# Sums of squares by one-column matmuls in two kinds of norm, and the first token half's output chain at a higher priority

## The chip, the core and the metric

The kernel runs on one core of a Trainium2 chip. A core has TensorE (PE in the profile; its weight loads are PEld), VectorE (DVE), ScalarE (ACT) and GpSimd (POOL), each with its own instruction queue that is worked in order, and DMA queues issued by SyncE (SP). Engines wait for each other by semaphores. The metric is the device time of one execution in microseconds (us); 3045.44 is the median of three runs of the kernel before.

## The reference

Three layers run one after the other on 512 tokens of width 1024. Each has a mixer and an MLP, and every one of them is wrapped in the same two norms:

```python
u = rms_norm(h, g[0])          # before the mixer (or MLP)
u = mixer(u)                   # layer 1: hybrid; 2: attention; 3: RWKV, a recurrent mixer
h = h + rms_norm(u, g[1])      # behind it, added to the residual
u = rms_norm(h, g[2])          # before the MLP, and so on

def rms_norm(x, g):
    return x * rsqrt(mean(x * x, axis=-1) + 1e-6) * g
```

The last step of the RWKV mixer is a product with a 1024x1024 matrix `w_o`; behind it come a norm, the residual, the next norm and the MLP of the third layer. The very first operation of the whole program is the norm of the input x.

## The kernel before

Activations lie transposed: eight tiles of 128 features by 512 tokens. Most products are computed from two parts, high and low, of either operand (`split`, and `load_w` for the weights: ACT casts the high part at line 63 or 69, DVE subtracts it at line 65 or 70), three matmuls each at line 80. Norms work on two halves of 256 tokens (`HALVES`), so that the second half's norm can lie beside products of the first.

A norm over features is a sum across partitions. `SumSq.add` squares a tile on ACT and adds it on DVE into an accumulator of 128x256 (`sqa`, lines 261 to 265). `sums` then multiplies each block of 128 tokens of the accumulator, as the weights, with a column of ones (line 272), so that tokens come to lie on partitions; DVE scales (line 274), POOL takes the power -1/2 (line 275). `rstd` broadcasts the factor over the partitions again by a product with the identity (line 281) and copies it out of PSUM (line 284). `postnorm` scales the mixer's output by it (line 185), adds it to h (187) and feeds a second `SumSq` with h for the next norm; `prenorm` scales h (172) and splits it.

Three places build a `SumSq`: `l1_start` (the norm of x; both halves are spawned at once, with the same priority), `out7` at the end of the RWKV mixer (the last of eight partial products with `w_o`, line 1228, is added to y at line 1230, and y is squared), and `final` for every other mixer and MLP. `out7` hands over to `postnorm` and to the next `prenorm`, for one half and then for the other.

The order of instructions on each engine is set by a scheduler when the program is built. It goes by a priority that code asks for with `high_priority` (`ahead`); the constants `HP...` on line 17 are those priorities, and `HPO` belongs to the chains of `out7`. At run time each engine works its list in that order: an instruction that waits holds up all behind it on its engine. PSUM for products and sums comes from one pool of four tiles (`psm`), the squares' tiles from two (four in `l1_start`).

Of the kernel before, what the change touches and what calls it, by code (L numbers as in the profile page):

```python
# [8 lines left out]
F32 = mybir.dt.float32  # L9
F32R = mybir.dt.float32r  # L10
AF = mybir.ActivationFunctionType
# [2 lines left out]
PSUM = bass.MemoryType.PSUM  # L14
DRAM = bass.MemoryType.DRAM

HP, HPA, HPB, HPS, HPO, HP1, HP1B = 300, 50, 50, -300, 0, 300, 300
S = 512
D = 1024
NT = D // 128  # L20
# [4 lines left out]
class Core:  # L25
# [147 lines left out]
            self.split(t, xn[i][0][:, s0:s1], xn[i][1][:, s0:s1])  # L173
        yield

    def postnorm(self, y, q, g, s0, s1):

        nc = self.nc
        q.sums()
        yield  # L180
        rs = q.rstd()
        q2 = SumSq(self, s1 - s0)
        for i in range(NT):
            t = self.tmp.tile([128, S], F32, tag="t", name="t")[:, :s1 - s0]
            nc.vector.scalar_tensor_tensor(t, y[i][:, s0:s1], self.vec(g, i), rs, ALU.mult, ALU.mult)
            hs = self.h[i][:, s0:s1]
            nc.vector.tensor_tensor(hs, hs, t, op=ALU.add)
            q2.add(hs)
            if i % 2:
                yield  # L190
        return q2
# [58 lines left out]
class SumSq:  # L250


    def __init__(self, core, n, pool=None):
        self.c, self.n, self.acc = core, n, None
        self.pool, self.bufs = (pool, 4) if pool else (core.tmp, 2)

    def add(self, a):
        c, nc = self.c, self.c.nc
        if self.acc is None:
            self.acc = c.tmp.tile([128, S // 2], F32, tag="sqa", name="sqa", bufs=2)[:, :self.n]  # L260
            nc.scalar.activation(self.acc, a, AF.Square)
        else:
            t = self.pool.tile([128, S // 2], F32, tag="sq", name="sq", bufs=self.bufs)[:, :self.n]
            nc.scalar.activation(t, a, AF.Square)  # L264
            nc.vector.tensor_tensor(self.acc, self.acc, t, op=ALU.add)  # L265

    def sums(self):
        c, nc = self.c, self.c.nc
        nb = self.n // 128
        ps = c.psm.tile([128, S], F32, tag="mm", name="mm")  # L270
        for b in range(nb):
            nc.tensor.matmul(ps[:, b:b + 1], self.acc[:, b * 128:(b + 1) * 128], c.ones[:, 0:1], start=True, stop=True)
        self.r = c.tmp.tile([128, 4], F32, tag="r1", name="r1", bufs=4)[:, :nb]
        nc.vector.tensor_scalar(self.r, ps[:, :nb], 1.0 / D, 1e-6, ALU.mult, ALU.add)  # L274
        nc.gpsimd.tensor_tensor(self.r, self.r, c.mhalf[:, :nb], op=ALU.pow)  # L275
# [35 lines left out]
class L1:  # L311


    def l1_start(self, pool, xn, g):

        x = pool.tile([128, NT, S], F32, name="x0")
        src = self.I["x"].rearrange("i p t -> p i t")
        self.h = [x[:, i] for i in range(NT)]
        for s0, s1 in HALVES:
            def chain(s0=s0, s1=s1):  # L320
                for n in (slice(0, 4), slice(4, 8)):
                    self.nc.sync.dma_start(x[:, n, s0:s1], src[:, n, s0:s1])
                q = SumSq(self, s1 - s0, pool)
                for i in range(NT):
                    q.add(self.h[i][:, s0:s1])
                yield from self.prenorm(q, g, xn, s0, s1)
            self.spawn(self.ahead(chain(), HP1 if s0 == 0 else HP1B))
        self.pump()
# [681 lines left out]
class L3:  # L1010
# [20 lines left out]
    def l3_mixer(self, u, g_post, then):  # L1031
        nc, tc, I = self.nc, self.tc, self.I
        W = lambda n, i: I[n][i]
        with ExitStack() as lx:
# [3 lines left out]
            with tc.tile_pool(name="mx", bufs=8) as mx:  # L1038
                c0 = lp.tile([128, 6 * NT], F32, name="c0")
                a, b = VEC_AT["mu_prev"], VEC_AT["mu_next"]  # L1040
# [42 lines left out]
                for s0, s1 in SEG3:  # L1083
# [3 lines left out]
                    for m in range(NT):  # L1087
                        ps = self.psm.tile([128, S], F32, tag="mm", name="mm")[:, :s1 - s0]
# [22 lines left out]
            y, out7 = self.rwkv(lp, rkd, vm, tw, ta, sg)  # L1111
            self.unspill_h()
            for s0, s1 in HALVES:
                self.spawn(self.ahead(out7(s0, s1, g_post, then), HPO))
                next(self.bg[-1])

    def spill_h(self):
# [10 lines left out]
    def rwkv(self, lp, rkd, vm, tw, ta, sg):  # L1128
        nc, tc, I = self.nc, self.tc, self.I
        with ExitStack() as cx:  # L1130
            pool = lambda n, b, **kw: cx.enter_context(tc.tile_pool(name=n, bufs=b, **kw))
# [17 lines left out]
            a = VEC_AT["k_a"]  # L1149
# [44 lines left out]
            y = [self.accp.tile([128, S], F32, tag="acc", name="y") for _ in range(NT)]  # L1194
# [27 lines left out]
                    yield  # L1222

            def out7(s0, s1, g_post, then):
                q = SumSq(self, s1 - s0)
                for m in range(NT):
                    ps = self.psm.tile([128, S], F32, tag="mm", name="mm")[:, :s1 - s0]
                    nc.tensor.matmul(ps, wo[NT - 1][:, m], ys[NT - 1][:, s0:s1], start=True, stop=True)
                    a = y[m][:, s0:s1]
                    nc.vector.tensor_tensor(a, a, ps, op=ALU.add)  # L1230
                    q.add(a)
                yield
                q = yield from self.postnorm(y, q, g_post, s0, s1)
                yield from then(q, s0, s1)

            def lora2(p, a, n):
# [298 lines left out]
            t = -4  # L1535
            while t <= 36 + (NQ - 1) * 16 or live or lf or fills:
                for st, at in ((2, 31), (1, 9), (0, 0), (3, -4)):
                    q, e = divmod(t - at, 16)
# [174 lines left out]
```

## Time and profile before

| what | value |
|---|---|
| median of three runs | 3045.44 us (3045.03 to 3048.03) |
| the profiled execution | 3048.25 us |
| its span in the profile | 3046.5 us |
| PE busy | 2872.4 us, 94% of the span |
| VectorE, ScalarE, POOL busy | 55%, 44%, 6% |
| adds into accumulators (line 265) | 182 of 424 ns, 75.6 us |

The span runs from the first instruction to the last; 1.75 us of the execution lie around it. A row of a timeline gives the start and the length in us, the engine, the line of the kernel, the operation, output and input by their names in the program, the shape, and how many equal instructions are merged into it; behind it in brackets the engine's idle time before it, with what ended it. A matmul of 32-bit floats that isn't split shows as two records.

### The profile page before, as it was taken

Reading aid. Unit: us, or ns where it says so; the run is one execution under the profiler, and the core shown is the slowest. Engines: PE = TensorE matmul, PEld = TensorE weight load, DVE = VectorE, ACT = ScalarE, POOL = GpSimd, SP = SyncE. Lnnn points to the kernel's source line nnn. Section 1 sums busy time; section 2 is a strip of 40 time slices with the busy share of each in tenths; the row PEclk is TensorE's granted clock in tenths of the full one; section 3 lists DMA queues with packets and bytes.
Section 4 is the critical chain, followed back from the end, with each engine's and each line's share of the span. In section 5 each row is a group of like instructions: output and inputs, shape, how many; then the busy total and the mean of one; then the engine's idle time right before and its main releaser. Section 6 shows DMA issues by size and latency. Waiting matters only on the chain.

```text
span 3046.5 us, 53309 instructions
## 1 busy us (share of the span) xinstructions
PE 2872.4 (94%) x21768; PEld 2330.7 (77%) x21768; DVE 1685.9 (55%) x3475; ACT 1337.1 (44%) x2489; POOL 168.1 (6%) x604
## 2 busy tenths in 40 slices
PE   7999999999999999899999999996889988699998
PEld 6877778778898888876988888765666666498887
DVE  5566684554462334767634445964566666653345
ACT  5565662673343223555533332644444444333222
POOL 0000000000000000000000000012222222000000
PEclk9999999999999999999999999997889998799999
DMA  4211122324223232221222242321111111212231
GB/s 138 95 42 50 42 85 90 101 73 137 95 77 99 95 97 97 75 79 49 91 83 96 91 132 96 101 69 22 25 33 38 42 34 28 91 57 96 97 105 41
DMA packets 140453, 234.74 MB, mean 77 GB/s; under 512 B 63088, under 2 KB 85360, under 8 KB 140080
## 3 DMA queue, kind: packets, MB, share of 16 engines
q1 hardware_dynamic: 137888, 229.40, 23.9%
q8 instruction: 171, 2.80, 0.4%
q10 hardware_dynamic: 2320, 1.93, 0.2%
q14 instruction: 74, 0.61, 0.1%
HBM read 220.72 MB, written 10.55 MB: 76 GB/s over the span
## 4 chain that ended last, share of the span: by engine, by line
PE 81%; DVE 9%; ACT 5%; issue 2%; DMA 1%; POOL 1%; SPq 1%; DVEq 0%; POOLq 0%; ACTq 0%
PE mm L80 58%; PE mm L1090 2%; PE fil L1204 2%; PE o L732 2%; PE mm L416 1%; PE mm L1310 1%; PE tr L722 1%; PE o L950 1%; PE mm L761 1%; PE mm L1454 1%; PE tr L924 1%; DVE sqa L265 1%; PE mm L903 1%; PE mm L1245 1%; PE mm L1511 1%
## 5 line engine op out<-in xcount | busy, mean ns | idle before, releaser
L80 PE MATMUL mm<-xh,wh 128*128 128x512 f32 (+1 forms) x2072 | 738.8, 358 | 10.4 <-ACT xh L69 6.3
L80 PE MATMUL mm<-xl,wh 128*128 128x512 f32 (+1 forms) x2072 | 736.5, 357 | 0.3 <-DVE xl L70 0.3
L80 PE MATMUL mm<-xh,wl 128*128 128x512 f32 (+1 forms) x2072 | 732.7, 355 | 2.1 <-DVE wl L65 2.1
L63 ACT CAST wh<-wr 128x1024 fp32r<-128x1024 f32 (+1 forms) x343 | 356.9, 1044 | 756.8 <-PE mm L80 613.9
L65 DVE TENSOR_TENSOR wl<-wr,wh 128x1024 fp32r<-128x1024 f32 (+1 forms) x343 | 416.6, 1217 | 460.9 <-ACT wh L63 451.2
L80 PEld LDWEIGHTS mm<-xh,wh 128*128 128x128 f32 x2072 | 392.5, 190 | 73.5 <-ACT xh L69 7.3
L80 PEld LDWEIGHTS mm<-xh,wl 128*128 128x128 f32 x2072 | 392.1, 190 | 60.3 <-issue 3.5
L80 PEld LDWEIGHTS mm<-xl,wh 128*128 128x128 f32 x2072 | 392.3, 190 | 56.7 <-issue 3.3
L80 PE MATMUL mm<-hl,wh 128*128 128x512 f32 (+1 forms) x880 | 305.9, 348 | 0.0
L80 PE MATMUL mm<-hh,wl 128*128 128x512 f32 (+1 forms) x880 | 304.5, 347 | 0.0
L80 PE MATMUL mm<-hh,wh 128*128 128x512 f32 (+1 forms) x880 | 304.5, 347 | 0.0
L80 PEld LDWEIGHTS mm<-hl,wh 128*128 128x128 f32 x880 | 167.3, 190 | 22.4 <-DVE hl L70 0.5
L80 PEld LDWEIGHTS mm<-hh,wl 128*128 128x128 f32 x880 | 167.2, 190 | 21.9
L80 PEld LDWEIGHTS mm<-hh,wh 128*128 128x128 f32 x880 | 166.9, 190 | 22.0
L241 DVE TENSOR_TENSOR acc<-acc,mm 128x256 f32<-128x256 f32 (+1 forms) x88 | 47.4, 542 | 179.1 <-PE mm L80 179.1
L265 DVE TENSOR_TENSOR sqa<-sqa,sq 128x256 f32<-128x256 f32 x182 | 75.6, 424 | 54.9 <-ACT sq L264 50.9
L1337 ACT COPY vs<-mm 64x256 f32<-64x256 f32 x64 | 23.4, 366 | 165.6 <-PE mm L1332 164.7
L275 POOL TENSOR_TENSOR r<-r,mhalf 128x2 f32<-128x2 f32 x24 | 23.0, 959 | 1299.5 <-DVE r L274 1299.5
L69 ACT CAST hh<-t 128x512 fp32r<-128x512 f32 (+1 forms) x106 | 57.0, 539 | 77.7 <-DVE t L212 68.6
L1310 PE MATMUL mm<-ar,bk 64*128 64x128 f32 x512 | 61.9, 369 | 29.0 <-DVE ar L1301 17.0
L674 DVE CUSTOM_DVE_ANT_0 s<-mm,cmask 128x128 f32<-128x128 f32 (+3 forms) x128 | 59.9, 487 | 46.8 <-PE mm L756 23.0
L1310 PEld LDWEIGHTS mm<-ar,bk 64*128 64x128 f32 x512 | 51.6, 258 | 40.3 <-issue 36.5
(407 smaller groups left out, 4945.0 us busy)
## 6 DMA issues: line engine op xcount, KB each, us to landing
wr<-in_mlp_w_dram SPq DMA_DIRECT2D x128, 512.0 KB, 3.5
wr<-in_w_ffn_in_dram SPq DMA_DIRECT2D x44, 512.0 KB, 3.5
wr<-in_w_mg_dram SPq DMA_DIRECT2D x24, 512.0 KB, 3.5
wr<-in_w_br_dram SPq DMA_DIRECT2D x24, 512.0 KB, 3.5
wr<-in_attn_w_in_dram SPq DMA_DIRECT2D x18, 512.0 KB, 3.5
wr<-in_w_ffn_out_dram SPq DMA_DIRECT2D x16, 512.0 KB, 3.5
wr<-in_w_kv_dram SPq DMA_DIRECT2D x12, 512.0 KB, 3.5
wr<-in_nsa_w_dram SPq DMA_DIRECT2D x8, 512.0 KB, 3.6
```

The lines of the kernel that those rows point to most:

```text
L63: nc.scalar.copy(hi, raw)
L65: nc.vector.tensor_tensor(lo, raw, hi.bitcast(F32), op=ALU.subtract)
L69: self.nc.scalar.copy(hi, src)
L80: nc.tensor.matmul(ps, l, r[:, s0:s1], start=(n == 0), stop=(n == 3 * nk - 1))
L241: nc.vector.tensor_tensor(a, a, ps, op=ALU.add)
L265: nc.vector.tensor_tensor(self.acc, self.acc, t, op=ALU.add)
L416: nc.tensor.matmul(ps[:, b % 2, :], l[:, t], r, start=(n == 0), stop=(n == 23))
L674: nc.vector.tensor_tensor_reduce(s, ps, mask, -1.0, 3e38, ADD, ALU.min, m)
L732: nc.tensor.matmul(po[hh * 64:hh * 64 + 64, c + x0:c + x1], vv[w][:, b, vo:vo + 64], pts[hh][w][:, b, x0:x1], start=(w + i == 0), stop=Fal ...
L1090: nc.tensor.matmul(ps, ws[m][:, i * 128:(i + 1) * 128], xr[i][:, s0:s1], start=(i == 0), stop=(i == NT - 1))
L1204: nc.tensor.matmul(ps, w[:, i * 128:(i + 1) * 128], vm[i], start=(i == 0), stop=(i == NT - 1))
L1310: nc.tensor.matmul(ps[h][:, c], bk[rw, cc].rearrange("p a t -> p (a t)"), ar[rw, :, cc * 64:(cc + 1) * 64], start=True, stop=True)
```

## The change

`SumSq` gets a second way (`pe=True`): every squared tile is multiplied with the column of ones as soon as it is there, two matmuls for the two blocks of 128 tokens, and PSUM adds them up over the eight tiles. The adds on DVE go, and `sums` has nothing more to multiply. Used in `l1_start`, in `out7` and in the norm of h behind `out7`, for both halves each: six norms, 6 x 7 adds less, 6 x 14 matmuls more. `final` stays as it was. `HPO` becomes 300, and holds for the first half alone; the second half's chain keeps 0.

```diff
-HP, HPA, HPB, HPS, HPO, HP1, HP1B = 300, 50, 50, -300, 0, 300, 300
+HP, HPA, HPB, HPS, HPO, HP1, HP1B = 300, 50, 50, -300, 300, 300, 300
...
-    def postnorm(self, y, q, g, s0, s1):
+    def postnorm(self, y, q, g, s0, s1, pe=False):
...
-        q2 = SumSq(self, s1 - s0)
+        q2 = SumSq(self, s1 - s0, pe=pe)
...
     def add(self, a):
         c, nc = self.c, self.c.nc
-        if self.acc is None:
+        if self.pe:
+            if self.m == 0:
+                self.ps = c.psm.tile([128, S], F32, tag="mm", name="mm")
+            t = self.pool.tile([128, S // 2], F32, tag="sq", name="sq", bufs=self.bufs)[:, :self.n]
+            nc.scalar.activation(t, a, AF.Square)
+            for b in range(self.n // 128):
+                nc.tensor.matmul(self.ps[:, b:b + 1], t[:, b * 128:(b + 1) * 128], c.ones[:, 0:1],
+                                 start=(self.m == 0 and b == 0), stop=(self.m == NT - 1), skip_group_check=True)
+            self.m += 1
+        elif self.acc is None:
...
-        ps = c.psm.tile([128, S], F32, tag="mm", name="mm")
-        for b in range(nb):
+        ps = self.ps if self.pe else c.psm.tile([128, S], F32, tag="mm", name="mm")
+        for b in range(0 if self.pe else nb):
...
-                q = SumSq(self, s1 - s0, pool)
+                q = SumSq(self, s1 - s0, pool, pe=True)
...
-                self.spawn(self.ahead(out7(s0, s1, g_post, then), HPO))
+                self.spawn(self.ahead(out7(s0, s1, g_post, then), HPO if s0 == 0 else 0))
...
-                q = SumSq(self, s1 - s0)
+                q = SumSq(self, s1 - s0, pe=True)
...
-                q = yield from self.postnorm(y, q, g_post, s0, s1)
+                q = yield from self.postnorm(y, q, g_post, s0, s1, pe=True)
```

The lists of POOL and SP stay as they are. Those of PE, DVE and ACT change at the start and at the end of the RWKV mixer only. (Lines behind 260 lie ten further down in the changed kernel; the sums are its line 266, the broadcast is 291, the products with `w_o` are 1238.)

PE at the start of the program, before: the sums of the first half, the broadcast of its factor (`ident` with `r`), the sums of the second half behind the first product of the layer.

```order
L272 MATMUL mm<-ones,sqa 128x1 x2
L281 MATMUL mm<-ident,r_177 128x128 x2
L80 MATMUL mm<-xh,wh 128x256
L272 MATMUL mm<-ones,sqa 128x1 x2
L80 MATMUL mm<-xh,wh 128x256
L80 MATMUL mm<-xl,wh 128x256
L80 MATMUL mm<-xh,wl 128x256
```

And now: eight tiles of the first half (two matmuls each), and eight of the second half in two groups between the first products; the second half's broadcast (`r_312`) comes behind three products instead of eighteen.

```order
L266 MATMUL mm<-ones,sq 128x1 x16
L291 MATMUL mm<-ident,r_184 128x128 x2
L80 MATMUL mm<-xh,wh 128x256
L266 MATMUL mm<-ones,sq 128x1 x8
L80 MATMUL mm<-xl,wh 128x256
L266 MATMUL mm<-ones,sq 128x1 x8
L80 MATMUL mm<-xh,wh 128x256
L291 MATMUL mm<-ident,r_312 128x128 x2
L80 MATMUL mm<-xl,wh 128x256
L80 MATMUL mm<-xh,wl 128x256
```

DVE at the same place, before: the adds, the first half's factor (`r_177`), the first weight's low part (`wl`) ahead of the scaling of x.

```order
L265 TENSOR_TENSOR sqa<-sqa,sq 128x256 x9
L274 TENSOR_SCALAR r_177<-mm 128x2
L265 TENSOR_TENSOR sqa<-sqa,sq 128x256 x5
L65 TENSOR_TENSOR wl<-wr,wh 128x1024
L172 SCALAR_TENSOR_TENSOR t<-x_148,vecs,rs 128x256 x3
```

And now: the scaling comes at once, and `wl` stands behind the factor of the second half (`r_312`).

```order
L284 TENSOR_SCALAR r_184<-mm 128x2
L172 SCALAR_TENSOR_TENSOR t<-x_148,vecs,rs 128x256 x3
L70 TENSOR_TENSOR xl<-t,xh 128x256 x3
L172 SCALAR_TENSOR_TENSOR t<-x_148,vecs,rs 128x256 x3
L70 TENSOR_TENSOR xl<-t,xh 128x256
L172 SCALAR_TENSOR_TENSOR t<-x_148,vecs,rs 128x256
L70 TENSOR_TENSOR xl<-t,xh 128x256 x3
L172 SCALAR_TENSOR_TENSOR t<-x_148,vecs,rs 128x256
L284 TENSOR_SCALAR r_312<-mm 128x2
L65 TENSOR_TENSOR wl<-wr,wh 128x1024
```

PE at the end of the RWKV mixer, before: sixteen products with `w_o` (eight of each half), the sums and the broadcast of the first half's norm, the sums and the broadcast of h for the next norm, and the MLP's first products.

```order
L1228 MATMUL mm<-ys,wr 128x256 x16
L272 MATMUL mm<-ones,sqa 128x1 x2
L281 MATMUL mm<-ident,r_26192 128x128 x2
L272 MATMUL mm<-ones,sqa 128x1 x2
L281 MATMUL mm<-ident,r_26266 128x128 x2
L80 MATMUL mm<-xh,wh 128x256
```

And now, first the beginning and then the second half's products. The first half's sums stand one by one between its products (tile 1 behind product 1, tile 2 behind product 5, then one by one); tiles 6 to 8 and the second half's first tile stand in the row with x8; the first half's broadcast (`r_26223`) follows the last product. The 24 behind it are the last four tiles of the second half and eight of h.

```order
L1238 MATMUL mm<-ys,wr 128x256
L266 MATMUL mm<-ones,sq 128x1 x2
L1238 MATMUL mm<-ys,wr 128x256 x4
L266 MATMUL mm<-ones,sq 128x1 x2
L1238 MATMUL mm<-ys,wr 128x256
```

```order
L1238 MATMUL mm<-ys,wr 128x256
L266 MATMUL mm<-ones,sq 128x1 x8
L1238 MATMUL mm<-ys,wr 128x256 x4
L266 MATMUL mm<-ones,sq 128x1 x2
L1238 MATMUL mm<-ys,wr 128x256
L266 MATMUL mm<-ones,sq 128x1 x2
L1238 MATMUL mm<-ys,wr 128x256
L266 MATMUL mm<-ones,sq 128x1 x2
L1238 MATMUL mm<-ys,wr 128x256
L291 MATMUL mm<-ident,r_26223 128x128 x2
L266 MATMUL mm<-ones,sq 128x1 x24
L291 MATMUL mm<-ident,r_26304 128x128 x2
```

What moved: the broadcast of the first half stood behind all sixteen products before, too, but the sums now stand among them, and the second half's sums of h come later, one tile at a time between products of the MLP.

## Rows read from the trace of the kernel before

**Rows 1.** The page: busy time of each engine, and the chain by engine.

```profile
PE 2872.4 (94%) x21768; PEld 2330.7 (77%) x21768; DVE 1685.9 (55%) x3475; ACT 1337.1 (44%) x2489; POOL 168.1 (6%) x604
...
PE 81%; DVE 9%; ACT 5%; issue 2%; DMA 1%; POOL 1%; SPq 1%; DVEq 0%; POOLq 0%; ACTq 0%
```

**Rows 2.** Busy time by stretch: stretch, its length, each engine, PEclk, DMA.

```profile
2760.00:3020.00 260.00, 260.00 (x1271) 217.37 (x1270) 108.98 (x144) 77.83 (x105) 0.69 (x1) 1.00 0.27 87
```

**Rows 3.** Timeline of the start: start, length, engine, line, operation.

```profile
5.81 1.01 ACT L264 ACTIVATE sq<-x 128x256 f32<-128x256 f32 x3
...
11.55 1.01 PE L272 MATMUL mm<-ones,sqa 128*128 128x1 f32 x4 [11.55 <-DVE sqa L265]
...
15.15 1.22 DVE L65 TENSOR_TENSOR wl<-wr,wh 128x1024 fp32r<-128x1024 f32 x1
...
16.28 1.27 DVE L172 SCALAR_TENSOR_TENSOR t<-x,vecs,rs 128x256 f32<-128x256 f32 x3
...
17.25 0.58 PE L80 MATMUL mm<-xh,wh 128*128 128x256 f32 x1 [2.30 <-ACT xh L69]
...
17.63 0.85 PE L272 MATMUL mm<-ones,sqa 128*128 128x1 f32 x4
...
18.70 0.41 PE L80 MATMUL mm<-xl,wh 128*128 128x256 f32 x1
...
21.05 0.41 PE L80 MATMUL mm<-xh,wl 128*128 128x256 f32 x1
...
21.61 0.28 PE L80 MATMUL mm<-xh,wl 128*128 128x256 f32 x1
...
22.25 0.71 PE L281 MATMUL mm<-ident,r 128*128 128x128 f32 x4 [0.25 <-POOL r L275]
```

**Rows 4.** Waits between 5 and 30 us: who waited for whom, total, times, longest.

```profile
PE mm L80 <- DVE wl L65: 0.8, 1, 0.8
```

**Rows 5.** Timeline of PE at the passage to the last MLP.

```profile
2629.91 9.86 PE L1228 MATMUL mm<-ys,wr 128*128 128x256 f32 x30 [1.66 <-DVE ys L1524]
...
2640.74 0.60 PE L272 MATMUL mm<-ones,sqa 128*128 128x1 f32 x4
2646.31 1.22 PE L281 MATMUL mm<-ident,r 128*128 128x128 f32 x4 [4.97 <-POOL r L275]
2657.45 1.01 PE L272 MATMUL mm<-ones,sqa 128*128 128x1 f32 x4 [9.92 <-DVE sqa L265]
...
2665.26 0.58 PE L80 MATMUL mm<-xl,wh 128*128 128x256 f32 x1 [0.28 <-DVE xl L70]
...
2686.22 0.60 PE L272 MATMUL mm<-ones,sqa 128*128 128x1 f32 x4 [1.26 <-DVE sqa L265]
```

**Rows 6.** Timeline of DVE and of POOL at the same passage.

```profile
2631.14 0.42 DVE L1230 TENSOR_TENSOR y<-y,mm 128x256 f32<-128x256 f32 x1 [0.24 <-PE mm L1228]
2632.00 0.42 DVE L1230 TENSOR_TENSOR y<-y,mm 128x256 f32<-128x256 f32 x1 [0.43 <-PE mm L1228]
...
2638.93 0.76 DVE L265 TENSOR_TENSOR sqa<-sqa,sq 128x256 f32<-128x256 f32 x2
...
2647.98 0.88 DVE L185 SCALAR_TENSOR_TENSOR t<-y,vecs,rs 128x256 f32<-128x256 f32 x2 [2.28 <-ACT rs L284]
...
2663.65 1.22 DVE L65 TENSOR_TENSOR wl<-wr,wh 128x1024 fp32r<-128x1024 f32 x1
...
2643.17 3.09 POOL L275 TENSOR_TENSOR r<-r,mhalf 128x2 f32<-128x2 f32 x1 [59.18 <-DVE r L274]
2658.74 1.60 POOL L275 TENSOR_TENSOR r<-r,mhalf 128x2 f32<-128x2 f32 x1 [12.48 <-DVE r L274]
```

**Rows 7.** Busy time by stretch at the passage, columns as in rows 2.

```profile
2636.00:2642.50 6.50, 5.04 (x23) 3.63 (x21) 6.40 (x20) 4.66 (x11) 0.00 (x0) 0.99 0.08 20
2643.00:2657.00 14.00, 1.22 (x4) 0.93 (x4) 11.72 (x29) 6.52 (x13) 3.09 (x1) 0.50 0.28 91
2657.00:2665.20 8.20, 3.88 (x14) 3.21 (x14) 5.93 (x12) 2.54 (x6) 1.60 (x1) 0.50 0.59 193
```

More of the change, by code (lines that the diff above doesn't have):

```diff
@@ L250, with __init__ @@
 class SumSq:
-    def __init__(self, core, n, pool=None):
+    def __init__(self, core, n, pool=None, pe=False):
         self.c, self.n, self.acc = core, n, None
+        self.pe, self.m = pe, 0
         self.pool, self.bufs = (pool, 4) if pool else (core.tmp, 2)
```

## The prediction, written before the changed kernel ran

> **What bounds the kernel now.** I read the page's busy times and its chain first: TensorE (PE) is busy for 94% of the span and 81% of the chain that ended last is its own [rows 1]. In a long stretch behind the recurrent mixer PE has no gap at all [rows 2]. So most of the kernel is one stream of matmuls, and a norm costs time only where that stream waits for it. The change touches two such places, which I read in the timeline, engine by engine: the start, until the first products of the layer stream without waiting, and the passage from the recurrent mixer (lines 1228 to 1234) into the last MLP. What follows each place is PE's stream, so a shift of the stream's beginning is carried to the end; the weight loads behind it are issued when PE, ScalarE or VectorE frees a buffer, and move along.
>
> At the start [rows 3] the squares begin on ScalarE at 5.8 us, the sums of the first half end on PE at 12.56, VectorE scales from 16.28 (one weight split of 1.22 us stands ahead of it) and PE's products run without a wait from 18.70. They are slow at first: the rows lengthen at 0.41 us and shorten to 0.28 about 21.5; these are the two clock levels, 1.2 and 2.4 GHz. At the passage [rows 5, 6] the last products of the mixer begin at 2629.91, the broadcast of the norm's factor at 2646.31, the sums of the next norm at 2657.45 and the unbroken stream at 2665.26. VectorE is full there: 11.72 of 14 us [rows 7]. The granted clock is 0.99 of full between 2636 and 2642.5, and 0.50 from 2643 until the stream has run for five microseconds, 2.4 and 1.2 GHz [rows 7].
>
> **What one sum costs on either engine.** An add into the accumulator takes VectorE 0.34 us start to start (one takes 0.42, two 0.76 [rows 6]). Its replacement is two one-column matmuls for each 128x256 square, which the trace shows as four records. The trace has this only once per norm: 1.01 us alone at the low clock, 0.85 behind another matmul [rows 3], 0.60 alone at the high one [rows 5]. I take 0.85 at the low level and half, 0.43, at the high. So per tile PE pays more than VectorE saved, at either level; six norms lose 42 adds (14 us of VectorE) and gain 84 matmuls (18 us of PE at the high level, 36 at the low). What counts is what stands behind them in PE's queue, which the order rows of the change show.
>
> The Trainium skill (TensorE: Matmul & The Clock Gate, section LDWEIGHTS) prices a weight load at its columns over 1.2 GHz: for 128 columns 107 ns, whatever the clock, so an estimate by it is 0.43 us a tile also at the low level. The rows at the low clock show twice that, and the measurement decides.
>
> **The start.** The first half's sums now follow its squares: eight tiles from 5.9 at 0.85 end at 12.7, where the adds and one sum ended at 12.56: nothing gained. The weight split ahead of the scaling goes, so scaling begins at 15.5 instead of 16.28. But ScalarE casts the first weight only after three casts of x, so PE's first product starts at about 18.2 instead of 17.25. Behind it PE's queue holds four tiles of the second half's sums (3.4 us, to 21.8), one product, four more tiles (to 25.4). On VectorE the split of the first weight stands behind the second half's factor, which waits for those sums: it ends at about 26.8, and the broadcast needs 1.3 us more (its power on POOL and four records). Products run without a wait from about 27.6: 8.9 later than 18.70. What comes back: the wait of 0.8 for a weight split [rows 4], and the second half's broadcast with the idle time before it, 0.75, which stood in the stream [rows 3]. The low clock at the stream's beginning costs about the same in both. Start: **+7.3 us**. If the clock were high during the sums, they would take 3.4 less and the stream would begin at the high clock (1.3 less): +2.6. These are the two ends.
>
> **The passage.** PE's queue now puts the sum of the first tile right behind the first product, and four products behind that. The first product's add starts at 2631.14 [rows 6]; add takes 0.42, the square as much, so PE stands until 2632.0, sums, and goes on at 2632.9 instead of 2630.8. Until the first half's last sum it has eight products and seven sums, each 0.85 at the low clock (the adds of y show 0.86 from product to product [rows 6]): 12.8, to 2645.7. The broadcast stands behind eleven more pieces (seven products, four sums of the second half) and a wait of about 1 us for the second half's first square: 2645.7 + 1.0 + 9.4 = 2656.1, against 2646.31. The factor's power on POOL hides under this. Scaling starts 1.7 later, at 2657.8. VectorE then has eight scalings and eight adds of h, 8 x (0.40 + 0.34) = 5.9 us without the seven sums, to 2663.7; the order puts the second tile of h last, so seven squares and their sums come after it, 0.4 and 7 x 0.85 = 6.0: 2670.5, where before the sums ended at 2658.46 (2657.45 + 1.01). From there to the stream it was 6.8 us. Two pieces of it go: the power took 1.60 beside a weight split [rows 6] and has VectorE idle now (the one at the far end of the bounds is 0.8 less), and a split of 1.2 between scaling and residual. So the stream starts at 2675.3, **+10.0**. Inside it, eight sum tiles at 0.43 stand where one stood (+3.0), while the hole of 1.26 before the second half's sums [rows 5] and its broadcast (0.5) leave it: +1.2. Passage: **+11.2 us**. With the clock high throughout, the fifteen pieces after 2632.9 and the eleven after them cost half, the stream starts about when it did and at the high clock: between -3 and +3, I take +1.
>
> A row on POOL bears on one term: the power took 3.09 us while VectorE ran two weight splits [rows 6]. The Trainium skill (SBUF — State Buffer, section SBUF: two separate sides) says VectorE with two SBUF inputs and a POOL operation exclude each other for a whole instruction; the trace agrees. By that rule the first power gets as long again in the change, which costs nothing behind eleven pieces, and the second gets short, which is the 0.8 above.
>
> The sum is 18.5 us on the profiled execution's 3048.25 (span 3046.5 and 1.75 around it). That execution stood 2.8 above the median of the runs, 3045.44; on the median it makes 3063.9, and I say 3063.
>
> **The cases.** Which clock the sums run at decides between the first three, since no row shows a long unbroken run of one-column matmuls. For the low one speaks that the clock stayed at 0.50 through the sums, broadcasts and single products from 2657 to 2665.2 [rows 7]; against it that those were not dense.
> 1. Sums at the low clock at both places: 3063. Chance 0.5.
> 2. Low at the start (+7), but the mixer's last products raise the clock as they did at 2636 and it falls again before the next norm: there the broadcast is 1.4 late, the sums after h take 6.0, the stream starts 2 to 4 late. +3.5 with what stands inside: 3056. Chance 0.2.
> 3. High during the sums at both places: +2.6 and +1, 3049. Chance 0.22.
> 4. Faster: VectorE was the full engine at the passage; 14 of its 28 removed adds lie in the first half's chain, 14 x 0.34 = 4.8, and the two waits at the start come back, 1.5: 3039. It needs the broadcast to leave PE as soon as the power is there; it decides for this case if eleven pieces ahead of it cost less than 0.3 us each, and a product alone showed 0.85 and 0.43. Chance 0.04.
> 5. The change does what it says and it doesn't show, because a load or another engine behind either place waited anyway: 3045. PE without a gap [rows 2] speaks against it. Chance 0.04.
>
> About 0.2%, 6.1 us, is what a measurement of this kernel can tell from no change. Slower by more (above 3051.5): cases 1 and 2 and a quarter of case 3, 0.75. Within: the rest of case 3 and case 5, 0.21. Faster: 0.04. The range holds cases 1 to 3, with 4 us beyond the first for where in the stream the clock rises: 3047 to 3068.
>
> **What would show it.** In the changed profile: PE's unbroken products at the start begin near 27 us (case 3: below 25), the sums stand between the first products; rows of the one-column matmuls step by 0.21 (low) or 0.11 (high). At the passage, counted from the mixer's last products, the broadcast comes 26 us after them instead of 16.4 (case 3: 17), the stream 45 instead of 35.4. It would be wrong if the broadcast came at 17 or sooner, or if PE ran later products while the first tile's sum waited.

## The result and the profile after

The changed kernel took 3069.63 us (median of six runs, 3066.01 to 3079.89) against 3046.39 (median of six, 3041.95 to 3051.58): a ratio of 1.0081, 95% interval 1.0065 to 1.0097, which is 24.7 us, 19.8 to 29.6. The forecast was slower, 3063 us and at most 3068, and its sum was 18.5 us; the measured time lies above its range. The profiled execution of the change took 3079.89 us, its slowest.

The page of the changed kernel answers to [rows 1]: PE has 40 us more, VectorE 14 less.

```profile
PE 2912.1 (95%) x21936; PEld 2367.2 (77%) x21936; DVE 1671.5 (54%) x3433; ACT 1338.7 (43%) x2489; POOL 169.1 (5%) x604
...
PE 82%; DVE 9%; ACT 5%; issue 2%; DMA 1%; POOL 1%; SPq 0%; ACTq 0%; DVEq 0%; POOLq 0%
```

PE's timeline at the start answers to [rows 3]. The sums of the first half end at 13.0; the second half's two groups of 3.41 us stand between the first three products; the unbroken products begin at 28.65 instead of 18.70 and run at the low clock (0.21 us from row to row) until 33.3.

```profile
6.01 6.99 PE L266 MATMUL mm<-ones,sq 128*128 128x1 f32 x32 [6.01 <-ACT sq L264]
14.05 1.22 PE L291 MATMUL mm<-ident,r 128*128 128x128 f32 x4 [1.04 <-POOL r L285]
18.43 0.58 PE L80 MATMUL mm<-xh,wh 128*128 128x256 f32 x1 [3.15 <-ACT wh L63]
18.80 3.41 PE L266 MATMUL mm<-ones,sq 128*128 128x1 f32 x16
22.07 0.56 PE L80 MATMUL mm<-xl,wh 128*128 128x256 f32 x1
22.43 3.41 PE L266 MATMUL mm<-ones,sq 128*128 128x1 f32 x16
25.70 0.56 PE L80 MATMUL mm<-xh,wh 128*128 128x256 f32 x1
27.77 1.23 PE L291 MATMUL mm<-ident,r 128*128 128x128 f32 x4 [1.51 <-POOL r L285]
28.65 0.56 PE L80 MATMUL mm<-xl,wh 128*128 128x256 f32 x1
```

PE at the passage answers to [rows 5]. PE waits 1.15 us for the first tile's square; the broadcast comes 24.2 us behind the first product (2646.63 to 2670.79), 16.4 before; the second norm's sums run in two pieces to 2685.1, most of it 28 records of 0.22 us each. At 2698.96 PE has waited 2.13 us inside the stream for a square of the second half, and the products behind it are slow again.

```profile
2646.63 0.67 PE L1238 MATMUL mm<-ys,wr 128*128 128x256 f32 x2 [1.66 <-DVE ys L1534]
2648.45 1.01 PE L266 MATMUL mm<-ones,sq 128*128 128x1 f32 x4 [1.15 <-ACT sq L264]
...
2659.71 2.56 PE L266 MATMUL mm<-ones,sq 128*128 128x1 f32 x12
2663.37 1.01 PE L266 MATMUL mm<-ones,sq 128*128 128x1 f32 x4 [1.11 <-ACT sq L264]
...
2670.79 0.61 PE L291 MATMUL mm<-ident,r 128*128 128x128 f32 x4
...
2678.98 6.13 PE L266 MATMUL mm<-ones,sq 128*128 128x1 f32 x28 [3.72 <-ACT sq L264]
2686.14 1.22 PE L291 MATMUL mm<-ident,r 128*128 128x128 f32 x4 [1.02 <-POOL r L285]
...
2690.08 0.56 PE L80 MATMUL mm<-xl,wh 128*128 128x256 f32 x1
...
2698.96 0.78 PE L266 MATMUL mm<-ones,sq 128*128 128x1 f32 x4 [2.13 <-ACT sq L264]
...
2701.88 0.85 PE L266 MATMUL mm<-ones,sq 128*128 128x1 f32 x4
...
2705.51 0.41 PE L80 MATMUL mm<-xh,wl 128*128 128x256 f32 x1
...
2706.24 0.28 PE L80 MATMUL mm<-xh,wh 128*128 128x256 f32 x1
```

Busy time by stretch there, columns as in [rows 2], the clock in the third column from the right. It is 0.53 of full while the first half's sums and products alternate, 0.96 for 6.5 us around the broadcast, 0.53 again through the sums of h and the single products after them. The stream begins at the low level and gets to the high one (0.82 on the mean up to 2696.80); the column still reads 1.00 through the wait of 2.13 us, and behind it 0.52 for 7 us.

```profile
2646.60:2668.00 21.40, 19.11 (x64) 16.50 (x64) 9.46 (x17) 6.89 (x14) 0.71 (x1) 0.53 0.33 102
2668.00:2674.50 6.50, 5.23 (x39) 4.91 (x37) 4.78 (x11) 4.55 (x9) 0.00 (x0) 0.96 0.32 93
2674.50:2690.00 15.50, 9.18 (x41) 8.72 (x42) 8.58 (x21) 5.41 (x13) 1.35 (x2) 0.53 0.26 96
2690.00:2696.80 6.80, 6.80 (x48) 6.62 (x47) 4.06 (x12) 2.47 (x7) 0.00 (x0) 0.82 0.01 2
2696.80:2699.00 2.20, 0.07 (x2) 0.04 (x1) 2.20 (x7) 1.50 (x4) 0.00 (x0) 1.00 0.00 0
2699.00:2706.00 7.00, 7.00 (x34) 7.00 (x35) 1.01 (x3) 0.42 (x1) 0.00 (x0) 0.52 0.00 0
2706.00:2720.00 14.00, 13.78 (x112) 13.18 (x112) 7.22 (x20) 5.64 (x14) 0.69 (x1) 1.00 0.01 2
```

The same instruction of both kernels, side by side, shows where the time went. ACT's copy of `yb` stands behind the start, its first `vs` at the head of the recurrent scan, a cast of `hh` behind the passage. First the kernel before:

```profile
152.06 0.59 ACT L771 COPY yb<-o 128x512 f32<-128x512 f32 x1 [0.57 <-PE o L736]
...
2037.11 1.52 ACT L1337 COPY vs<-mm 64x256 f32<-64x256 f32 x4 [8.56 <-PE mm L1332]
...
2807.92 0.62 ACT L69 CAST hh<-t 128x512 fp32r<-128x512 f32 x1 [1.39 <-DVE t L212]
```

And the changed kernel:

```profile
160.76 0.59 ACT L781 COPY yb<-o 128x512 f32<-128x512 f32 x1 [0.53 <-PE o L746]
...
2046.42 1.53 ACT L1347 COPY vs<-mm 64x256 f32<-64x256 f32 x4 [8.56 <-PE mm L1342]
...
2839.25 0.62 ACT L69 CAST hh<-t 128x512 fp32r<-128x512 f32 x1 [1.39 <-DVE t L212]
```

The start costs 8.7 us (160.76 - 152.06), 0.6 are added on the way to the scan (9.3), the first product of the passage is 16.7 late (2646.63 against 2629.91 in [rows 5]), the cast 31.3. So 7.4 us were lost in the scan, which the change doesn't touch, and 14.6 in the passage and the stream behind it.

### The profile page after: what moved, and what is told of

It is laid out like the page before. It is cut to its first block, busy times and chain, and to the rows that moved or that the text cites. A ratio compares the mean times of both kernels' runs of the same rounds, so it can differ in the third digit from the quotient of the medians.

```text
span 3078.1 us, 53602 instructions
## 1 busy us (share of the span) xinstructions
PE 2912.1 (95%) x21936; PEld 2367.2 (77%) x21936; DVE 1671.5 (54%) x3433; ACT 1338.7 (43%) x2489; POOL 169.1 (5%) x604
## 4 chain that ended last, share of the span: by engine, by line
PE 82%; DVE 9%; ACT 5%; issue 2%; DMA 1%; POOL 1%; SPq 0%; ACTq 0%; DVEq 0%; POOLq 0%
PE mm L80 56%; PE mm L1100 2%; PE fil L1214 2%; PE o L742 1%; PE mm L1320 1%; PE mm L426 1%; PE tr L732 1%; PE o L960 1%; PE mm L266 1%; PE mm L771 1%; PE fil L1227 1%; PE mm L1464 1%; PE mm L1255 1%; PE tr L934 1%; PE mm L913 1%
## 5 line engine op out<-in xcount | busy, mean ns | idle before, releaser
L275 DVE TENSOR_TENSOR sqa<-sqa,sq 128x256 f32<-128x256 f32 x140 | 57.9, 423 | 49.0 <-ACT sq L274 45.7
```

## The experiments

Each kernel was compared with the kernel before in five rounds. The table has the ratio with its interval, the same in us, the start's shift in the profile (the median over ACT's instructions between 150 and 175 us; ten kernels with an unchanged start have -1.9 to 0.0), and three distances from the first product of the passage: to the broadcast, to the first of a run of unbroken products, and to the 24th cast of `hh`, the row above. "Inside" is the last less the one before it. The ratio comes from all executions of a kernel, the other columns from the one that was profiled.

| kernel | ratio | us | start | broadcast | stream | 24th cast | inside |
|---|---|---|---|---|---|---|---|
| before | | | 0 | 16.4 | 35.4 | 178.0 | 142.7 |
| the change | 1.0081 (1.0065 to 1.0097) | +24.7 | +8.7 | 24.2 | 43.5 | 192.6 | 149.2 |
| control | 0.9995 (0.9982 to 1.0007) | -1.5 | -1.4 | 16.0 | 35.0 | 177.0 | 142.0 |
| start alone | 1.0043 (1.0027 to 1.0058) | +13.1 | +6.2 | 16.4 | 35.3 | 178.0 | 142.7 |
| passage alone | 1.0044 (1.0029 to 1.0060) | +13.4 | -1.5 | 24.4 | 43.7 | 192.5 | 148.9 |
| priority alone | 1.0015 (1.0006 to 1.0024) | +4.6 | -0.8 | 10.6 | 34.4 | 177.0 | 142.6 |
| passage, no priority | 1.0037 (1.0022 to 1.0051) | +11.3 | -1.2 | 18.8 | 35.6 | 184.1 | 148.5 |
| start, first half | 1.0040 (1.0026 to 1.0054) | +12.2 | +6.1 | 14.7 | 33.6 | 178.1 | 144.5 |
| start, sums twice | 1.0075 (1.0063 to 1.0087) | +22.9 | +21.1 | 15.7 | 34.6 | 177.5 | 142.9 |
| late x | 1.0054 (1.0041 to 1.0066) | +16.5 | +13.3 | 15.4 | 34.4 | 177.5 | 143.1 |
| start, second half behind | 1.0070 (1.0057 to 1.0083) | +21.3 | +9.4 | 14.7 | 33.6 | 176.5 | 142.9 |
| norm behind w_o alone | 1.0018 (1.0009 to 1.0027) | +5.5 | -0.5 | 19.3 | 38.6 | 179.3 | 140.8 |
| norm of h alone | 1.0044 (1.0030 to 1.0058) | +13.4 | -1.9 | 12.5 | 35.5 | 188.0 | 152.5 |
| passage, first half | 1.0031 (1.0020 to 1.0041) | +9.4 | -1.9 | 22.0 | 46.2 | 188.1 | 141.9 |
| change less second h | 1.0056 (1.0044 to 1.0068) | +17.1 | +7.8 | 24.3 | 43.6 | 184.6 | 141.0 |
| second h alone | 1.0037 (1.0023 to 1.0051) | +11.3 | 0.0 | 11.6 | 35.3 | 184.9 | 149.5 |
| second half late | 1.0017 (1.0007 to 1.0027) | +5.2 | -0.6 | 12.1 | 40.0 | 180.8 | 140.8 |

### The parts of the change

**Start alone.** Diffs are against the changed kernel where nothing else is said. The passage goes back:

```diff
-                q = SumSq(self, s1 - s0, pe=True)
+                q = SumSq(self, s1 - s0)
-                q = yield from self.postnorm(y, q, g_post, s0, s1, pe=True)
+                q = yield from self.postnorm(y, q, g_post, s0, s1)
-                self.spawn(self.ahead(out7(s0, s1, g_post, then), HPO if s0 == 0 else 0))
+                self.spawn(self.ahead(out7(s0, s1, g_post, then), 0))
```

> The sums on TensorE in the norm of x alone; the rest as before. Theory (what stands behind a sum in PE's queue is delayed): the two profiles show the start 8.7 us later, so the time is 8 to 10 us above the kernel before, ratio 1.0026 to 1.0033, and the recurrent scan behind it is as long as before within a few us. Rival B (a later start changes the clock in the recurrent scan, which was 8 us longer in the changed kernel's profile): 14 to 17 us above. Rival C (the priority costs, not the sums): below 3 us.

Measured +13.1 us (8.2 to 17.7); its profile has the same rows to 28.6 as the change, but the clock rises at 30.5 instead of 33.3, and the shift is 6.2. The 8 to 10 us of the theory are at the lower end of the interval; rival C is out. The profiled scan was long again (586 us), so rival B stayed open.

**Passage alone:**

```diff
-                q = SumSq(self, s1 - s0, pool, pe=True)
+                q = SumSq(self, s1 - s0, pool)
```

> The sums on TensorE at the end of the recurrent mixer and in the norm of h behind it, with the priority of the first half; the norm of x as before. Theory: the profiles show 14 us between the mixer's last products and the second half's end, so 13 to 16 us above the kernel before (ratio 1.0043 to 1.0053), and this and the start alone add up to the whole change (about 24). Rival B: about 8, since the scan takes the rest. Rival C: 13 to 16 as well, but then the priority alone shows it too.

Measured +13.4 (8.8 to 18.3), as expected. With the start alone it makes 26.5, the change 24.7: within the intervals the two add up.

**Priority alone**, all sums on VectorE:

```diff
-                q = SumSq(self, s1 - s0, pool, pe=True)
+                q = SumSq(self, s1 - s0, pool)
-                q = SumSq(self, s1 - s0, pe=True)
+                q = SumSq(self, s1 - s0)
-                q = yield from self.postnorm(y, q, g_post, s0, s1, pe=True)
+                q = yield from self.postnorm(y, q, g_post, s0, s1)
```

> Only the priority: HPO 300 for the first half's chain, 0 for the second, with all sums as before. Theory: PE's order in the passage is the same as before, so within 2 us of the kernel before. Rival C: 5 us or more slower.

Measured +4.6 (1.8 to 7.3), which the theory missed; the interval reaches into rival C's range. PE's order up to the MLP's first products is that of before, VectorE's isn't, and the passage isn't longer: in its profile the broadcast leaves 5.8 us sooner, but then PE waits 17 us for VectorE's adds, and the rest stands where it stood. PE's timeline there:

```profile
2637.79 0.71 PE L291 MATMUL mm<-ident,r 128*128 128x128 f32 x4 [1.04 <-POOL r L285]
2655.52 1.01 PE L282 MATMUL mm<-ones,sqa 128*128 128x1 f32 x4 [17.02 <-DVE sqa L275]
```

Its profiled run was its fastest, 2 us under the median of the kernel before. Where its other runs lost their 4 to 6 us no profile shows.

**Passage without the priority:** the passage alone, and

```diff
-                self.spawn(self.ahead(out7(s0, s1, g_post, then), HPO if s0 == 0 else 0))
+                self.spawn(self.ahead(out7(s0, s1, g_post, then), 0))
```

> The passage's sums on TensorE with HPO 0 for both halves, as before; the norm of x as before. Theory: PE's order is that of the passage with the priority but for single pieces, so within 3 us of it, 13 to 16 above the kernel before. Rival C: no more than 8 above.

Measured +11.3 (6.7 to 15.5), about as with it and below the 13 to 16 expected. PE's order in the passage is the same as in the passage alone; VectorE's and ACT's differ in a few places. In its profile the clock rose among the first half's products, not behind them: the broadcast came 2.4 us late instead of 8.0, the stream 0.3. So the same sums on PE took 6.1 us more than before in this profile and 14.5 in that of the passage alone; up to the broadcast the difference stands in the length of PE's rows, at one level or the other. The comparisons, over several executions each, don't show such a difference. Its timeline of PE has a tile at 0.36 us start to start where the change has 0.71:

```profile
2638.35 0.50 PE L266 MATMUL mm<-ones,sq 128*128 128x1 f32 x4
2638.71 0.68 PE L1238 MATMUL mm<-ys,wr 128*128 128x256 f32 x2
...
2650.76 0.61 PE L291 MATMUL mm<-ident,r 128*128 128x128 f32 x4
```

**Control:** the priority alone, and

```diff
-HP, HPA, HPB, HPS, HPO, HP1, HP1B = 300, 50, 50, -300, 300, 300, 300
+HP, HPA, HPB, HPS, HPO, HP1, HP1B = 300, 50, 50, -300, 0, 300, 300
```

> The changed file with every sum on VectorE and HPO 0: on each engine the order of the kernel before, in another build. Theory: within 2 us of the kernel before; what is left over in the priority-alone run (4 us) is then more than a build costs. If this too is 3 to 5 us above, that is what two builds of the same order differ by, and as much of each other run is not the change.

Measured -1.5 (-5.5 to 2.1): another build of the same order costs nothing that can be measured.

### What costs the start

**First half on TensorE, second on VectorE:** the start alone, and

```diff
-                q = SumSq(self, s1 - s0, pool, pe=True)
+                q = SumSq(self, s1 - s0, pool, pe=s0 == 0)
```

> In the norm of x the first half's sums on TensorE, the second half's on VectorE as before; the rest as before. Theory (the second half's sum tiles in PE's queue, and the weight split behind the second half's factor, cost the start): nothing stands ahead of the weight split now, so products run without a wait from about 19 to 20 us instead of 28.6, and the time is 0 to 2 us above the kernel before. Rival D (the slow one-column sums of the first half cost it): 5 us or more above.

Measured +12.2 (7.9 to 16.5): the number is rival D's, and the theory was wrong in what it left out. ACT's squares are paced by PE's slow sums (each waits some 0.44 us for a free tile), and ACT's list now has the first weight's cast behind the copy of the factor and three casts of x: in its timeline it comes at 17.8 instead of 13.47. VectorE's split of that weight stands behind eight `xl`. PE waits for both:

```profile
18.89 0.58 PE L80 MATMUL mm<-xh,wh 128*128 128x256 f32 x1 [3.28 <-ACT wh L63]
...
23.52 0.58 PE L80 MATMUL mm<-xh,wl 128*128 128x256 f32 x1 [3.83 <-DVE wl L65]
```

**Each sum's two matmuls issued twice**, on the start alone, the second pair into columns that nobody reads:

```diff
+            for b in range(self.n // 128):
+                nc.tensor.matmul(self.ps[:, 2 + b:3 + b], t[:, b * 128:(b + 1) * 128], c.ones[:, 0:1],
+                                 start=False, stop=(self.m == NT - 1), skip_group_check=True)
```

> The start alone with the sums on TensorE, each sum's two matmuls issued twice (the second pair into columns that nobody reads). Theory (PE works its queue in order, and each tile of sums takes 0.85 us at the low clock): eight tiles more before the first factor and eight before the second, 6.8 us each, so the unbroken products begin at 28.6 + 13.6 = 42 us and the time is 12 to 14 us above the start alone. Rival E (the wait is VectorE's, for the order of its scalings, and the sums lie beside it): 0 to 6 us above the start alone.

PE's timeline, from the first tile to the last of the first half, and the beginning of the unbroken products:

```profile
5.89 1.01 PE L266 MATMUL mm<-ones,sq 128*128 128x1 f32 x4 [5.89 <-ACT sq L264]
...
18.71 0.99 PE L269 MATMUL mm<-ones,sq 128*128 128x1 f32 x4
...
42.19 0.56 PE L80 MATMUL mm<-xl,wh 128*128 128x256 f32 x1
```

The unbroken products begin at 42.19, as forecast to 0.2 us, and the shift rises by 14.9 (6.2 to 21.1). The comparison gives 22.9 (19.2 to 26.5), 9.8 above the start alone, where 12 to 14 was expected; rival E is out. In the profile what stands in PE's queue is paid in full; the comparison shows less, and why is open.

**The first weight's parts ahead:** the start alone, and

```diff
-HP, HPA, HPB, HPS, HPO, HP1, HP1B = 300, 50, 50, -300, 300, 300, 300
+HP, HPA, HPB, HPS, HPO, HP1, HP1B = 300, 50, 50, -300, 300, 300, 0
```

> The start alone with the sums on TensorE, and the second half's chain of x at priority 0 instead of 300: ScalarE's first weight cast and VectorE's first weight split then stand ahead of the scalings, and the second half's sums behind fifteen products. Theory (not the sums of the first half cost the start, but what the order puts ahead of the first weight's parts): unbroken products begin at 17 to 20 us instead of 28.6, the eight tiles of the second half stand in the stream at 0.43 to 0.85 each, 3.4 to 6.8: 2 to 6 us above the kernel before, 6 or more below the start alone. Rival D (the slow sums cost it wherever they stand): within 3 us of the start alone.

Measured +21.3 (17.4 to 25.3): 8 above the start alone, past both. The first product came at 17.6, about where it did before, but the second half's eight tiles then stood among products at the low clock and took 6.4 us there, the products ran unbroken from 30.4, and the second half's factor came at 35.3:

```profile
17.61 0.58 PE L80 MATMUL mm<-xh,wh 128*128 128x256 f32 x1 [1.71 <-ACT xh L69]
...
21.84 2.55 PE L266 MATMUL mm<-ones,sq 128*128 128x1 f32 x12
...
27.17 3.41 PE L266 MATMUL mm<-ones,sq 128*128 128x1 f32 x16
...
35.26 0.61 PE L291 MATMUL mm<-ident,r 128*128 128x128 f32 x4
```

This profile's shift is 9.4; the comparison is twice that. What the rest is stays open.

**Late x.** On the control:

```diff
-                    self.nc.sync.dma_start(x[:, n, s0:s1], src[:, n, s0:s1])
+                    for _ in range(4 if s0 == 0 and n.start == 0 else 1):
+                        self.nc.sync.dma_start(x[:, n, s0:s1], src[:, n, s0:s1])
```

> All sums on VectorE and HPO 0, and the first quarter of x is loaded four times one after the other (the same data into the same place), so the whole program begins some microseconds late and does nothing else differently. It tests rival B: does a later start make the recurrent scan longer? Theory: no; the time rises by what the start of the profile shows (about 6 us), the scan takes 576 to 586 us as in all kernels so far. Rival B: 3 to 6 us more than the start shows, as the start alone (7.4 us in its profile, 11.8 in the comparison) and the half of it (7.2 and 13.9) seemed to say.

The delay was larger than meant: the start's shift is 13.3, 14.3 against the mean of the unchanged starts (-1.0). The comparison gives 16.5 (12.5 to 20.1) and the scan took 579 us. A later start by itself does not make the scan longer by more than the interval can hide, which is against rival B. Over all seventeen profiles, whose order in the scan is the same, the scan (first to last `vs`) took 573 to 586 us, 576 to 586 where the start was changed (583 or more in five of seven), up to 585 where it wasn't (583 or more in one of ten). What makes a scan long stays open.

### What costs the passage

The first three are edits of the passage alone.

**The norm behind w_o alone:**

```diff
-                q = yield from self.postnorm(y, q, g_post, s0, s1, pe=True)
+                q = yield from self.postnorm(y, q, g_post, s0, s1)
```

> Of the passage, the norm behind w_o alone has its sums on TensorE (with the priority), the norm of h has them on VectorE. Theory: the broadcast comes 19 to 24 us after the mixer's last products began instead of 16.4 (by where the clock rises among the eleven pieces ahead of it), VectorE has its seven adds of h's norm back, and the second half's sums inside the stream are one piece again: the stream starts 3 to 8 us late, 3 to 8 above the kernel before. Rival: the norm of h is what costs, and this one is within 2.

**The norm of h alone:**

```diff
-                q = SumSq(self, s1 - s0, pe=True)
+                q = SumSq(self, s1 - s0)
```

> Of the passage, the norm of h alone has its sums on TensorE (with the priority), the norm behind w_o has them on VectorE. Theory: the broadcast is not late (17 or sooner); the first half's sums come after h in one run of 32 records, 3.4 to 6.9 us by the clock, for 5 to 6 us of adds that VectorE no longer does: 0 to 3 us; the second half's eight pieces inside the stream wait for their squares and cost 1 to 6 us with the clock that they may lose: 2 to 8 above the kernel before.

**The first half alone:**

```diff
-                q = SumSq(self, s1 - s0, pe=True)
+                q = SumSq(self, s1 - s0, pe=s0 == 0)
-                q = yield from self.postnorm(y, q, g_post, s0, s1, pe=True)
+                q = yield from self.postnorm(y, q, g_post, s0, s1, pe=s0 == 0)
```

> The passage with the sums of the first half alone on TensorE in both norms (with the priority), the second half's on VectorE. Theory: the eight pieces of the second half inside the stream go, with the idle time before them (2.1 us) and the low clock behind it (3.5 us): 3 to 6 us less than the whole passage's 11, so 5 to 8 above the kernel before. Rival: what is ahead of the broadcast is all that costs, and this is 10 to 12 above as well.

They measured +5.5 (2.7 to 8.2), +13.4 (9.1 to 17.7) and +9.4 (6.1 to 12.5). The first and the last are as expected or little above, and the second is above its range; in its profile nearly all of it is in the column "inside". Where the second half's sums of h are one piece, it is 140.8 to 143.1 (144.5 once, in start, first half, whose passage is that of before); where they are eight, 148.5 to 152.5. Ahead of the stream the sums cost between 0 and 11 us. With the sums of the norm behind w_o on TensorE, the stream comes 0.3 and 3.2 us late in the two profiles where the clock rose among the first half's products, 8.1 to 10.8 in the four where it rose behind them.

The 144.5 is worth a look. In start, first half, the one sum stands in the stream behind a wait of 1.31 us, and 1.5 us behind it the products fall to 0.21 us from row to row for 3.4 us. Eleven other profiles have the same wait of 1.26 to 1.31 us there and keep their rows of 0.12. PE's timeline in start, first half:

```profile
2697.64 0.61 PE L282 MATMUL mm<-ones,sqa 128*128 128x1 f32 x4 [1.31 <-DVE sqa L275]
...
2700.03 0.41 PE L80 MATMUL mm<-xh,wh 128*128 128x256 f32 x1
```

**The change less the second half's sums of h:**

```diff
-                q = yield from self.postnorm(y, q, g_post, s0, s1, pe=True)
+                q = yield from self.postnorm(y, q, g_post, s0, s1, pe=s0 == 0)
```

> The change as it is, but for one norm: the second half's sums of h are on VectorE again (three halves of the passage's four and the norm of x stay on TensorE). Theory (the term of the forecast that failed is the one inside the stream, +1.2 forecast, 6.6 in the profile of the change): the eight pieces, the idle time before them and the low clock behind it go, so 5 to 8 us below the change, some 17 to 19 above the kernel before. Rival F (the stream's begin was worth more than 10 us and the inside nothing): within 3 us of the change, 22 to 25 above before.

**These sums alone:** the norm of h alone, and

```diff
-                q = yield from self.postnorm(y, q, g_post, s0, s1, pe=True)
+                q = yield from self.postnorm(y, q, g_post, s0, s1, pe=s0 > 0)
```

> Only the second half's sums of h on TensorE (with the priority), all other sums on VectorE. Theory: the stream begins where it did (34 to 36 us after the mixer's last products), and inside it 6 to 10 us are lost: 6 to 10 above the kernel before. Rival F: 1 to 2 above.

Taken out of the change these eight pieces give back 7.6 us (24.7 to 17.1, the 17 to 19 expected), and the inside falls from 149.2 to 141.0. Put into the kernel before they leave the stream's beginning where it was (35.3) and cost 11.3 (7.0 to 15.5), a little above the 6 to 10 expected; inside, 6.8 more than before. The seven executions of this last kernel stand in two groups, four at 3050 to 3054 us and three at 3063 to 3064; the profiled one is of the upper, with a scan of 585 us. Rival F is out. PE's timeline shows the term in it by itself: the wait of 2.40 us, then slow rows; in [rows 5] a wait of 1.26 for the one sum stood ahead of 0.60.

```profile
2684.25 0.61 PE L266 MATMUL mm<-ones,sq 128*128 128x1 f32 x4 [2.40 <-ACT sq L264]
...
2685.88 0.85 PE L266 MATMUL mm<-ones,sq 128*128 128x1 f32 x4
2686.59 0.56 PE L80 MATMUL mm<-xl,wh 128*128 128x256 f32 x1
...
2691.63 0.61 PE L266 MATMUL mm<-ones,sq 128*128 128x1 f32 x4
```

### An attempt at a faster version

**Second half late:** the priority alone, and

```diff
-                next(self.bg[-1])
+                if s0 == 0:
+                    next(self.bg[-1])
```

> All sums on VectorE as before, the priority as in the change, and the second half's last products with w_o are not issued right behind the first half's but later, among the first products of the MLP. Theory (VectorE was the bound of the passage before: 15 adds of the second half, 15 x 0.37 = 5.6 us, stood in the first half's chain): the stream starts some 6 us sooner after the mixer's last products (29 instead of 35.4), 4 to 7 us below the kernel before. Rival: the second half's chain is then late and PE waits for it inside the stream, no gain.

Measured +5.2 (2.1 to 8.2), where 4 to 7 us less than before was expected. The broadcast came 4.3 us sooner, but VectorE's time was filled with weight splits, and the eight products came back among the first products of the MLP at the low clock: the unbroken ones begin at 40.0. No version beat the kernel before.

## Why the prediction was too low

**The direction** was right for the reason given: the sums went from an engine that had gaps into the queue of the one that has none, at a price per tile above the add's. The rows are case 1, low clock and 0.85 us a tile, at the start and for most of the passage; in the passage the clock rose for 6.5 us and fell again before the sums of h, as case 2 has it, but later than case 2 put it.

**The start** was forecast at +7.3, with products from 27.6. They came at 28.65, with the low clock up to 33.3 where "about the same in both" was assumed (4.7 us of slow products instead of 2.7 in [rows 3]). Shift 8.7, 7.1 to 9.7 in the three profiles with this start against the mean of unchanged ones. Mis-sized by 1.4 in this profile.

**The passage up to the stream** was forecast at +10.0 and measured +8.1: broadcast 24.2 us behind the first product (26 forecast), stream 43.5 (45), since the clock rose for 6.5 us around the broadcast, which the sum had left out. The sum also has a slip: 2663.7, 0.4 and 6.0 make 2670.1 and not 2670.5, so that its own terms give +9.6. The order that it read was right: the second tile of h comes last, and 28 records in a row behind it.

**Inside the stream** is the step that failed. The forecast said: "eight sum tiles at 0.43 stand where one stood (+3.0), while the hole of 1.26 before the second half's sums and its broadcast (0.5) leave it: +1.2". Measured +6.5 (149.2 against 142.7), and 5.8 to 9.8 in the other four kernels with these eight pieces. The hole did not leave; it moved. The first tile's sum stands behind 48 products of the layer, where the single sum stood behind 144, and its square isn't there yet: 2.13 + 0.21 of waiting instead of 1.26, +1.1 where -1.26 was forecast. Behind that wait the clock fell: the 39 products up to the third tile took 7.5 us where the rows behind it give 4.8 for as many, +2.7 where nothing was forecast. The eight tiles took 1.35 (two, at the low level) and 2.5 us (six, at the high one), 3.4 more than the one, where 3.0 was forecast. Less the broadcast's 0.5 that is 6.7, for 6.5 measured. What was overlooked is that the wait moves to an earlier place and grows, and that the clock can fall behind it. In the kernel before it did not:

```profile
2686.00:2700.00 14.00, 13.77 (x113) 13.54 (x114) 9.23 (x24) 6.75 (x17) 0.69 (x1) 1.00 0.01 2
```

In all five profiles with the eight pieces the sum's wait was 2.13 to 2.50 us and the products behind it slow; of the twelve with one piece, with 1.26 to 1.31, one. The eight pieces' wait is longer and also stands sooner behind the stream's slow beginning (9 to 13 us instead of 19 to 21), and no run separates the two; that the clock falls because of the wait is read from these rows and not shown by an edit. That the eight pieces cost what they do is shown by the two kernels that take them out and put them in.

With these sizes the sum is 8.7 + 8.1 + 6.5 = 23.3 on the profiled execution, the comparison's 24.7. Of the 6.2 us between 18.5 and 24.7, the inside of the stream is 5.3, the start 1.4, the passage -1.9; 1.4 are in no stage. That the sum comes so near is partly luck: in most single kernels the two are further apart. The 7.4 us that the scan lost in the changed kernel's profile belong to that execution (it is 10 us above its median); other kernels with the same scan show it and the reverse.

**Two readings of the forecast.** At the low level 28 records of the sums took 6.13 us, 0.22 each, as the forecast's 0.85 a tile has it. The estimate by the Trainium skill (TensorE: Matmul & The Clock Gate, section LDWEIGHTS), 107 ns for a load of 128 columns, does not agree with that. The first power on POOL took 0.71 us, though a weight split began on VectorE 0.17 after it; the timelines of DVE and of POOL in the changed kernel:

```profile
2662.71 1.22 DVE L65 TENSOR_TENSOR wl<-wr,wh 128x1024 fp32r<-128x1024 f32 x1
...
2662.54 0.71 POOL L285 TENSOR_TENSOR r<-r,mhalf 128x2 f32<-128x2 f32 x1 [60.53 <-DVE r L284]
```

By the Trainium skill (SBUF — State Buffer, section SBUF: two separate sides) the one that starts first has the port for its whole instruction and the other is blocked; the forecast made this power long by that, though in the change the power started first. The split behind it took its usual 1.22 us, so these rows show no exclusion. Nothing hung on it. The later powers, which the forecast made 0.8 shorter, did get short: two of them took 1.35 us together.

**What stays open:** in most single kernels the comparison is 2 to 7 us above what start and passage show in their one profile, and in the second half behind 12 to 13. The scan's length, 573 to 586 us, varies as much; which runs have which length there can't be seen without their profiles.

## What to carry to other kernels

Before work moves to the engine that is the bound, price it there by a row at the clock it will run at, and look at what stands behind it in that queue; the adds it replaced cost less and lay beside other work. A sum split into eight pieces is also eight waits, and the first of them stands earlier than the whole did: look for its input at its new place. In a stream without gaps, price a wait also with slow rows behind it: here they followed every wait of more than 2 us in the stream, and one of the twelve of 1.3.

## What the runs showed of the chip

- One-column matmuls with 128x128 weights run one record every 0.21 to 0.22 us at the low clock and about 0.12 at the high one; 64 of them in a row, from 5.89 to 19.70 us without a gap (start, sums twice), ran at the low one to the end.
- At the start the clock column of the stretches stands at 1.00 (28.60 to 33.30 us in the changed kernel) while the rows of 128x256 products are 0.21 us apart; only the rows tell the level there.
- With the same order on PE the passage's sums cost 6.1 us where the clock rose early in it and 14.5 where it rose late; the passage of before took 176.5 to 178.1 us to the same cast in the eight profiles that have its sums and its second half in their old place.
